# Seven expert groups instead of nine in the last mixture-of-experts layer of a two-block network

## Chip, cores and metric

The kernel runs on one core of one Trainium2 chip. The metric is the device time in microseconds (us) of one execution; the figure for a kernel is the median of its runs.

## What is computed

The program runs a first block of two layers (neighbourhood attention with a Fourier mixer, then a retention mixer, each followed by a mixture of experts) and a second block of one layer (windowed attention, a gated scan and projections) over 256 tokens of 1024 numbers; the first layer also carries 256 context tokens. The part that matters here is the mixture of experts of the second layer, which sees the 256 tokens alone:

```python
def moe_ffn(tok, router_w, router_b, w1, w3, w2):
    T = tok.shape[0]
    scores = jax.nn.sigmoid((tok @ router_w).astype(jnp.float32))
    biased = (scores + router_b.astype(jnp.float32)).reshape(T, N_GROUPS, EXPERTS_PER_GROUP)
    group_score = lax.top_k(biased, TOP_K)[0].sum(axis=-1)
    g_sel = jnp.argmax(group_score, axis=-1)
    ...
    for e in range(N_EXPERTS):
        hid = jax.nn.silu(tok @ w1[e]) * (tok @ w3[e])
        out = out + gate[:, e:e + 1] * (hid @ w2[e])
    return out
```

Each token goes to two of 16 experts (512 places in all). An expert has w1 and w3 of 1024 x 512 and w2 of 512 x 1024 in float32, 6 MB together, and all 16 experts' weights are read once: 96 MB.

## The kernel before

`moe_late` (L1288 on) is the last layer's mixture of experts. It doesn't multiply every token by every expert. Tokens are gathered into rows of a 128-row tile, the products are made for the tile, and the result rows are added back to their tokens. A table, `GROUPS[1]` (L42 to L45), says which experts share a tile and how many of its 128 rows each has. Experts 14 and 15 are fixed: they have places of their own whatever the router says. The other 14 stand by rank: 0 is the expert with most tokens, 13 the one with fewest, found at run time (`ranking`, L1485 on). Before, the table has nine groups: 15 alone with 128 rows, 14 alone with 128 rows, ranks 0 and 13 with 96 and 32, ranks 1 and 12 with 96 and 32, and five pairs with 64 and 64. `CAPS` (L47) keeps the row count of each rank. If an expert has more tokens than rows, `overflow` (L1532 on) runs a loop over all 16 experts under a branch (L1548) that all engines test; it computes the rows that found no place.

Work on a group goes like this. `loads` (L1300) issues its weights on SP's queue: for each of w1, w3 and w2, in two halves, one load of 1 MB for each expert of the group, so a single expert has 6 loads, a pair 12, and a group of three has 18. `expert_load` takes the place of a ranked expert from a register that SP reads from the tile `order` (`places_of`, L1480 to L1483); experts 14 and 15 need no register. The tiles of the loads come from a ring of 11 buffers of 1 MB (3 kept through the program, and 8 of this stage), so load n + 11 can start when the matmuls on load n are done. On TensorE, `products` (L1396 to L1404, the matmul is L1403) goes through a half of a weight in steps of 128 rows of the contraction. At each step it multiplies column blocks of the stationary tokens with the weights of the experts they belong to; the block is as wide as the group's smallest expert (`columns`, L1389): one block of 128 columns for a single expert, two of 64 for a pair of 64s, four of 32 for 96 and 32. So a group is six units: two halves of w1, two of w3 and two of w2, and each unit uses one load for each expert of the group.

Around the products of a group lie, on TensorE, the gather of the next batch's tokens (L1382, four chunks of 8 matmuls for a batch), the slot numbers (L1357), the transposes of the hidden rows (L280) and the scatter of the group before (L1409) into four accumulators. `BATCHES` (L46) says which groups are gathered together, at most two. The weights of the first two groups (`first`, L1306, the first `NS` = 2 groups, 12 loads) are issued ahead of the router. `overflow` is called when group 1 is done, `bias_setup` of the block behind (L1737 on; it writes a table to memory and copies it there, L1759) when group 2 is done. After the last group come the last scatter, the residual and statistics (L1605, L493), and the second block's first product (L220).

Of the kernel before, what the change touches and what calls it, by code (L numbers as in the profile page):

```python
# [18 lines left out]
P = 128  # L19
# [19 lines left out]
NS = 2  # L39
one, two = lambda r: ((r, 128),), lambda a, b: ((a, 64), (b, 64))  # L40
SPLIT = (0, 2, 4, 7, 10, 12)
GROUPS = ((one(15), one(14), one(0), two(8, 13), one(1), one(2), two(9, 12), one(3), one(4), two(10, 11), one(5),  # L42
           one(6), one(7)),
          (one(15), one(14), ((0, 96), (13, 32)), ((1, 96), (12, 32)), two(2, 11), two(3, 10), two(4, 9), two(5, 8),
           two(6, 7)))  # L45
BATCHES = ((0, 1), (2, 3), (4, 5), (6, 7), (8,))  # L46
CAPS = [[dict(x for g in gs for x in g)[r] for r in range(16)] for gs in GROUPS]  # L47


# [81 lines left out]
class Kern:  # L131
# [1156 lines left out]
    def moe_late(self, ss):  # L1288
# [4 lines left out]
        with ExitStack() as es:  # L1293
# [6 lines left out]
            def loads(g):  # L1300

                rs = [r for r, _ in GR[g]]
                return [[load(name, r, u, n, c) for r in rs]
                        for name, n, c in (("moe_w1", 8, 512), ("moe_w3", 8, 512), ("moe_w2", 4, 1024)) for u in range(2)]

            first = [loads(g) for g in range(NS)]  # L1306
            tl, places, gates, rows, nat = self.route(l, ss, rp)
            self.holds = []
            pos, posm = places()
# [15 lines left out]
            def batch(gs):  # L1325
                oh, w = choose(gs)
                return wp.tile([P, KC, 256], F32, tag="xe", name=self.name("xe")), oh, w

            cur = batch(BATCHES[0])
            pm, oi, ranked = self.ranking(tl, pos, NT, lambda: tl([NT, 16, 16]))  # L1330
            ranked(place, posm, V)
            rows()
            g, den = gates()
# [17 lines left out]
            def slots(g, oh, a):  # L1351

                ex = GR[g]
                sp = self.psum((P, 2, 4))
                for i, (r, _) in enumerate(ex):
                    for t in range(NT):
                        nc.tensor.matmul(sp[:, i], oh[:, t, a:a + P], pr4[:, r, t, :], start=t == 0, stop=t == NT - 1)  # L1357
                st = wp.tile([P, 4], F32, tag="slot", name=self.name("slot"))
                a = 0
                for i, (r, n) in enumerate(ex):  # L1360
                    for b in range(a, a + n, 32):

                        c = b + (n if n in (64, 128) else 32)
                        if n in (64, 128) and b > a:
                            continue
                        V.tensor_copy(st[b:c], sp[b:c, i])
                    a += n
                fg = wp.tile([P, 2], F32, tag="fg", name=self.name("fg"))
                V.tensor_scalar(out=fg[:, 0:1], in0=st[:, 1:2], scalar1=-4096.0, scalar2=4096.0, op0=OP.mult, op1=OP.add)
                V.tensor_tensor(out=fg[:, 0:1], in0=fg[:, 0:1], in1=st[:, 0:1], op=OP.add)  # L1370
                V.tensor_tensor(out=fg[:, 1:2], in0=st[:, 2:3], in1=st[:, 3:4], op=OP.add)
                back = wp.tile([P, N], F32R, tag="back", name=self.name("back"))
                V.tensor_scalar(out=back, in0=iota, scalar1=fg[:, 0:1], scalar2=None, op0=OP.is_equal)
                return fg[:, 1:2], back

            def gather(x, oh, w, c):

                ps = self.psum((P, 2, 256))
                for j in range(2):
                    k = 2 * c + j  # L1380
                    for i in range(2 * NT):
                        nc.tensor.matmul(ps[:, j, 0:w], nat[i % 2][:, i // 2, k * P:(k + 1) * P], oh[:, i // 2, 0:w],  # L1382
                                         start=i == 0, stop=i == 2 * NT - 1)
                if c % 2:
                    V.tensor_copy(x[:, 2 * c:2 * c + 2, 0:w], ps[:, :, 0:w])
                else:
                    nc.scalar.activation(x[:, 2 * c:2 * c + 2, 0:w], ps[:, :, 0:w], AF.Copy)
# [8 lines left out]
            def products(outs, lhs, ws, g):  # L1396

                m = ws[0][0].shape[1]
                for u, we in enumerate(ws):
                    for k in range(m):  # L1400
                        for c, ps in enumerate(outs):
                            for a, b, e in columns(g):
                                nc.tensor.matmul(ps[a:b], lhs(u * m + k)[:, a:b], we[e][:, k, 512 * c:512 * c + 512],  # L1403
                                                 start=u == k == 0, stop=u == len(ws) - 1 and k == m - 1)  # L1404

            def scatter(y, back, start, stop):
                for k in range(KC):
                    for i in range(2):
                        nc.tensor.matmul(acc[k // 2][:, k % 2], y[i][:, k * P:(k + 1) * P], back,  # L1409
                                         start=start and k % 2 == i == 0, stop=stop and i == 1, skip_group_check=True)  # L1410
# [3 lines left out]
            todo = None  # L1414
            for bi, gs in enumerate(BATCHES):
                x, oh, _ = cur
                nxt = batch(BATCHES[bi + 1]) if bi + 1 < len(BATCHES) else None
                chunks = list(range(4)) if nxt else []
                for i, g in enumerate(gs):
                    if g >= NS:  # L1420
                        self.places_of(order, oi, GR[g])
                    ws = loads(g) if g >= NS else first[g]
                    xs = lambda k: x[:, k, P * i:P * i + P]
                    h1 = self.psum()
                    products([h1], xs, ws[0:2], g)
                    hs = wp.tile([P, 512], F32, tag="hid", name=self.name("hid"))
                    nc.scalar.activation(hs, h1, AF.Silu)
                    if chunks:
                        gather(*nxt, chunks.pop(0))
                    h3 = self.psum()  # L1430
                    products([h3], xs, ws[2:4], g)
                    V.tensor_tensor(out=hs, in0=hs, in1=h3, op=OP.mult)
                    if todo:
                        scatter(*todo, g == 1, False)
                    gate, back = slots(g, oh, P * i)
                    if len(gs) == 1 and chunks:
                        gather(*nxt, chunks.pop(0))
                    tp = self.psum((P, 4, P))
                    for j in range(4):

                        self.T(tp[:, j, :], hs[:, j::4])
                    hT = wp.tile([P, 4, P], F32, tag="hh", name=self.name("hh"))
                    nc.scalar.activation(hT, tp, AF.Copy)
                    while chunks and (len(gs) == 1 or len(chunks) > 2 * (1 - i)):
                        gather(*nxt, chunks.pop(0))
                    yp = [self.psum() for _ in range(2)]
                    products(yp, lambda k: hT[:, k], ws[4:6], g)
                    y = [wp.tile([P, D], F32R, tag=f"y{j}", name=self.name("y")) for j in range(2)]
                    for c in range(2):
                        s = slice(512 * c, 512 * c + 512)  # L1450
                        nc.scalar.activation(y[0][:, s], yp[c], AF.Copy, scale=gate)
                        V.scalar_tensor_tensor(out=y[1][:, s], in0=yp[c], scalar=gate, in1=y[0][:, s].bitcast(F32),
                                               op0=OP.mult, op1=OP.subtract)
                    todo = y, back
                    if g == 1:
                        c4 = lambda a: a.rearrange("p (k c) -> p k c", c=P)
                        t1 = lambda tag, w: wp.tile([P, w], F32, tag=tag, name=self.name("ov"))
                        room = (c4(t1("y0", D)), t1("y1", D), c4(t1("ovm", 256)), t1("hid", 512), c4(t1("hh", 512)),
                                t1("back", 256), t1("ovs", 64), rp.tile([P, 2, 512], F32, name="ovw"))
                        self.overflow(l, N, NT, cnt, pk, nat, acc, hs[:, 0:1], room, wp)  # L1460
                    if g == 2:
                        with self.pool("bias", 1) as bp:
                            self.bias_setup(bp)
                cur = nxt
# [612 lines left out]
```

## Time and profile before

| | |
|---|---|
| median of 3 runs | 1736.21 us (1733.53 to 1737.06) |
| profiled execution | 1734.04 us, its span 1732.3 us |
| TensorE (PE) busy | 1636.9 us, 94% of the span |
| VectorE, ScalarE, GpSimd busy | 50%, 37%, 15% |
| weight loads of the experts (both layers) | 192 of 1 MB |
| stage of the last layer's experts | from about 1024 us to 1281 us of the span |

The profile is one execution, seen by the hardware's records. Busy time says how long an engine worked, not what the end waited for. So the page's 40 slices show where the stage lies, the table of busy time by stretch shows each group with its DMA share and GB/s, the timeline of TensorE shows what runs in which order and how long, and the queue's own waits show what the loads wait for. A granted clock of 1.00 is TensorE at 2.4 GHz, 0.50 is 1.2 GHz.

### The profile page before, as it was taken

To read this page: it belongs to the slowest core of one execution; us is meant where nothing else is said; L and a number is where in the kernel's file an instruction comes from. 1 tells how busy PE (TensorE), PEld (TensorE's weight loads), DVE (VectorE), ACT (ScalarE), POOL (GpSimd) and SP (SyncE) were. 2 spreads that over 40 slices of the span, in tenths; PEclk is the share of its full clock that TensorE was granted. 3 is DMA by queue.
4 is the path that set the end of the run, shared out by engine and by line. 5 is a ranking of instruction groups with operands and counts; after the bars stand their busy time and mean duration, and the time that the engine had idled before them with its cause. 6 is when DMAs were issued, how large, how long until landed. Compare 5 with 4: busy or idle time off the path is not lost.

```text
span 1732.3 us, 26549 instructions
## 1 busy us (share of the span) xinstructions
PE 1636.9 (94%) x10640; PEld 1222.9 (71%) x10640; DVE 874.4 (50%) x1676; ACT 643.6 (37%) x1008; POOL 266.0 (15%) x265
## 2 busy tenths in 40 slices
PE   5999999988999998999999989999989999999999
PEld 3676657665555455879899955343449999999899
DVE  6565554573424346644555442111135756677665
ACT  3343333333423244433434331010135555655543
POOL 2212101221111111201211020000012110123300
PEclk8999999898999999999999989999989999999999
DMA  9644654477999987354433467999975454433360
GB/s 312 151 134 147 209 187 167 147 311 254 400 384 380 394 326 282 121 194 148 147 122 122 146 252 239 410 420 420 420 257 179 141 159 161 160 122 122 122 214 25
DMA packets 179230, 390.00 MB, mean 225 GB/s; under 512 B 25063, under 2 KB 141864, under 8 KB 149850
## 3 DMA queue, kind: packets, MB, share of 16 engines
q1 hardware_dynamic: 173882, 375.83, 60.1%
q0 software_dynamic: 4336, 10.99, 2.4%
q8 instruction: 87, 1.43, 0.3%
q10 hardware_dynamic: 880, 1.38, 0.2%
q14 instruction: 45, 0.37, 0.1%
HBM read 381.50 MB, written 14.85 MB: 229 GB/s over the span
## 4 chain that ended last, share of the span: by engine, by line
PE 66%; DVE 6%; issue 2%; ACT 2%; POOL 1%; DMA 1%; POOLq 0%; ACTq 0%; DVEq 0%
PE ps L220 12%; PE ps L221 12%; PE ps L222 12%; PE ps L1403 11%; PE ps L1174 8%; PE ps L280 3%; PE ps L1382 1%; DVE wl L211 1%; PE ps L1409 1%; DVE X L1956 1%; PE ps L408 1%; PE ps L1970 1%; DMA w<-in_moe_w_dram 1%; PE ps L1858 0%; PE ps L1839 0%
## 5 line engine op out<-in xcount | busy, mean ns | idle before, releaser
L211 DVE TENSOR_TENSOR wl<-w,wh 128x1024 fp32r<-128x1024 f32 x278 | 346.3, 1261 | 167.3 <-ACT wh L208 165.8
L208 ACT ACTIVATE wh<-w 128x1024 fp32r<-128x1024 f32 x280 | 290.9, 1056 | 200.2 <-PE ps L221 93.1
L220 PE MATMUL ps<-wh,xh 128*128 128x256 f32 x512 | 146.7, 286 | 1.6 <-DVE qk L553 1.6
L221 PE MATMUL ps<-wl,xh 128*128 128x256 f32 x512 | 144.8, 283 | 0.0
L222 PE MATMUL ps<-wh,xl 128*128 128x256 f32 x512 | 144.7, 283 | 0.0
L1403 PE MATMUL ps<-w,xe 128*64 128x512 f32 (+2 forms) x640 | 136.8, 595 | 0.0
L1174 PE MATMUL ps<-w,xe 128*64 128x512 f32 (+1 forms) x320 | 103.6, 596 | 1.2 <-DMA w<-in_moe_w_dram 1.2
L220 PE MATMUL ps<-x,wh 128*128 128x256 f32 x352 | 102.3, 291 | 0.0
L220 PEld LDWEIGHTS ps<-wh,xh 128*128 128x128 f32 x512 | 98.1, 192 | 5.7 <-issue 2.7
L221 PE MATMUL ps<-x,wh 128*128 128x256 f32 x352 | 99.8, 283 | 0.0
L222 PE MATMUL ps<-x,wl 128*128 128x256 f32 x352 | 99.8, 283 | 0.0
L221 PEld LDWEIGHTS ps<-wl,xh 128*128 128x128 f32 x512 | 98.2, 192 | 0.2
L222 PEld LDWEIGHTS ps<-wh,xl 128*128 128x128 f32 x512 | 98.2, 192 | 0.0
L1403 PEld LDWEIGHTS ps<-w,xe 128*64 128x64 f32 (+2 forms) x640 | 43.4, 131 | 72.9 <-issue 70.4
L220 PE MATMUL ps<-xh,wh 128*128 128x512 f32 (+1 forms) x224 | 83.2, 380 | 3.4 <-ACT xh L541 3.0
L221 PE MATMUL ps<-xl,wh 128*128 128x512 f32 (+1 forms) x224 | 82.7, 371 | 1.6 <-DVE xl L542 1.1
L222 PE MATMUL ps<-xh,wl 128*128 128x512 f32 (+1 forms) x224 | 81.4, 364 | 0.9 <-DVE wl L211 0.9
L1174 PEld LDWEIGHTS ps<-w,xe 128*64 128x64 f32 (+1 forms) x320 | 38.3, 158 | 57.5 <-issue 54.6
L220 PEld LDWEIGHTS ps<-x,wh 128*128 128x128 f32 x352 | 67.1, 191 | 1.4
L221 PEld LDWEIGHTS ps<-x,wh 128*128 128x128 f32 x352 | 67.3, 191 | 1.2 <-issue 0.2
L220 PE MATMUL ps<-wh,xp 128*128 128x256 f32 x224 | 65.5, 292 | 2.3 <-ACT xp L1659 2.3
L222 PEld LDWEIGHTS ps<-x,wl 128*128 128x128 f32 x352 | 67.2, 191 | 0.4
(472 smaller groups left out, 3669.8 us busy)
## 6 DMA issues: line engine op xcount, KB each, us to landing
w<-in_moe_w_dram SPq DMA_DIRECT2D x192, 1024.0 KB, 11.6
w<-in_w_in_dram SPq DMA_DIRECT2D x48, 1024.0 KB, 5.0
w<-in_ada_w_dram SPq DMA_DIRECT2D x40, 1024.0 KB, 5.1
w<-in_ret_w_in_dram SPq DMA_DIRECT2D x24, 1024.0 KB, 5.2
w<-in_mixab_w_in_dram SPq DMA_DIRECT2D x10, 1024.0 KB, 6.2
w<-in_ada_w_dram SPq DMA_DIRECT2D x16, 512.0 KB, 8.4
w<-in_ret_w_out_dram SPq DMA_DIRECT2D x8, 1024.0 KB, 5.1
w<-in_mixab_w_out_dram SPq DMA_DIRECT2D x4, 1024.0 KB, 7.4
```

The costliest lines, as they stand in the source:

```text
L208: nc.scalar.activation(hi, t[:, b:b + hk], AF.Copy)
L211: eng.tensor_tensor(out=lo, in0=t[:, b:b + hk], in1=hi.bitcast(F32), op=OP.subtract)
L220: mm(ps, lh, rh, start=start, stop=False, skip_group_check=skip)
L221: mm(ps, lh, rl, start=False, stop=False, skip_group_check=skip)
L222: mm(ps, ll, rh, start=False, stop=stop, skip_group_check=skip)
L280: self.nc.tensor.transpose(out, in_, self.ident[:n, :n])
L408: nc.tensor.matmul(ps[32 * j:32 * j + 32, :], self.S[:, kc, :], w[:, j * 512:(j + 1) * 512], start=kc == 0, stop=kc == KC - 1)
L1174: nc.tensor.matmul(ps[a], x[0][:, q, a], t[:, k, s], start=first, stop=last)
L1382: nc.tensor.matmul(ps[:, j, 0:w], nat[i % 2][:, i // 2, k * P:(k + 1) * P], oh[:, i // 2, 0:w], start=i == 0, stop=i == 2 * NT - 1)
L1403: nc.tensor.matmul(ps[a:b], lhs(u * m + k)[:, a:b], we[e][:, k, 512 * c:512 * c + 512], start=u == k == 0, stop=u == len(ws) - 1 and k == ...
L1409: nc.tensor.matmul(acc[k // 2][:, k % 2], y[i][:, k * P:(k + 1) * P], back, start=start and k % 2 == i == 0, stop=stop and i == 1, skip_gr ...
L1956: mul = lambda e, o, i1: e.tensor_tensor(out=o, in0=o, in1=i1, op=OP.mult)
```

## The change

The table for the last layer has seven groups. The two fixed experts are a pair with 64 rows each. Rank 0 and rank 13 stay with 96 and 32. Rank 1 has 64 rows and shares its tile with ranks 12 and 11, 32 rows each; rank 2 has 64 rows and shares with ranks 10 and 9, 32 rows each. Ranks 3 to 8 make three pairs. The first batch is the first group alone, and the loads issued ahead of the router are those of the first group, again 12. Slot numbers have room for three experts.

```diff
-          (one(15), one(14), ((0, 96), (13, 32)), ((1, 96), (12, 32)), two(2, 11), two(3, 10), two(4, 9), two(5, 8),
-           two(6, 7)))
-BATCHES = ((0, 1), (2, 3), (4, 5), (6, 7), (8,))
+          (two(15, 14), ((0, 96), (13, 32)), ((1, 64), (12, 32), (11, 32)), ((2, 64), (10, 32), (9, 32)), two(3, 8),
+           two(4, 7), two(5, 6)))
+BATCHES = ((0,), (1, 2), (3, 4), (5, 6))
...
-            first = [loads(g) for g in range(NS)]
+            first = loads(0)
...
-                sp = self.psum((P, 2, 4))
+                sp = self.psum((P, 3, 4))
...
-                    if g >= NS:
+                    if g:
                         self.places_of(order, oi, GR[g])
-                    ws = loads(g) if g >= NS else first[g]
+                    ws = loads(g) if g else first
```

On SP's queue, where the loads are issued, the twelfth load (w_8804 is the last of the 12 that are issued ahead of the router) is followed by the branch on the overflow count (cnti). Before:

```order
L192 DMA w_8802<-in_moe_w_dram 128x2048
L192 DMA w_8804<-in_moe_w_dram 128x2048
L1546 TENSOR_LOAD cnti_9211
L1546 ISA x2
L1548 COMPARE_AND_BRANCH
```

The change, at the same place:

```order
L192 DMA w_8802<-in_moe_w_dram 128x2048
L192 DMA w_8804<-in_moe_w_dram 128x2048
L1482 TENSOR_LOAD order_8884
L192 ISA
L192 DMA w_9179<-in_moe_w_dram 128x2048
```

Twelve loads with a rank's register (two reads of `order`) now stand between the twelfth load and the branch. The branch comes behind the 24th load, in the change:

```order
L192 DMA w_9199<-in_moe_w_dram 128x2048
L192 ISA
L192 DMA w_9201<-in_moe_w_dram 128x2048
L1546 TENSOR_LOAD cnti_9379
L1546 ISA x2
L1548 COMPARE_AND_BRANCH
```

On TensorE, at the first group's first product (ps_9037 before, ps_9039 now) and the gather behind it, before:

```order
L1382 MATMUL ps_9017<-oh_8866,nat_8856 128x256
L1403 MATMUL ps_9037<-w_8782,xe_8871 128x512 x4
L1403 MATMUL ps_9037<-w_8784,xe_8871 128x512 x4
L1382 MATMUL ps_9048<-oh_9027,nat_8855 128x256
L1382 MATMUL ps_9048<-oh_9027,nat_8856 128x256
```

The change, from the second half of the same product on:

```order
L1403 MATMUL ps_9039<-w_8786,xe_8871 64x512
L1403 MATMUL ps_9039<-w_8788,xe_8871 64x512
L1403 MATMUL ps_9039<-w_8786,xe_8871 64x512
L1403 MATMUL ps_9039<-w_8788,xe_8871 64x512
L1382 MATMUL ps_9058<-oh_9027,nat_8855 128x256
L1382 MATMUL ps_9058<-oh_9027,nat_8856 128x256
```

Each step of the contraction is now a matmul of 64 columns for each of two experts, so one unit uses two loads where it used one.

## Rows read from the trace of the kernel before

**Rows 1.** The page: its head, and parts of its 40 slices.
```profile
span 1732.3 us, 26549 instructions
...
PE   5999999988999998999999989999989999999999
...
DMA  9644654477999987354433467999975454433360
```

**Rows 2.** Busy time by stretch, one for each group: busy (count), clock, DMA share, GB/s.
```profile
1024.00:1048.30 24.30, 23.57 (x73) 12.01 (x73) 5.03 (x20) 3.78 (x6) 1.43 (x4) 1.00 0.59 203
1048.30:1076.30 28.00, 27.65 (x105) 15.52 (x104) 7.00 (x29) 3.88 (x7) 0.00 (x0) 1.00 0.77 255
1076.30:1107.60 31.30, 30.18 (x231) 10.75 (x230) 5.36 (x15) 3.17 (x5) 0.57 (x1) 1.00 0.87 352
1107.60:1136.50 28.90, 27.77 (x233) 11.28 (x232) 5.37 (x20) 3.17 (x5) 0.56 (x1) 1.00 1.01 410
1136.50:1165.50 29.00, 27.87 (x137) 12.23 (x136) 3.90 (x10) 3.17 (x5) 0.00 (x0) 1.00 1.01 420
1165.50:1194.50 29.00, 27.87 (x137) 12.24 (x136) 4.40 (x14) 3.17 (x5) 0.00 (x0) 1.00 1.01 420
1194.50:1224.60 30.10, 28.97 (x138) 12.36 (x137) 3.63 (x10) 2.95 (x5) 0.00 (x0) 1.00 1.01 420
1224.60:1254.60 30.00, 28.86 (x138) 12.29 (x137) 3.63 (x10) 2.95 (x5) 0.00 (x0) 1.00 1.01 420
1254.60:1280.80 26.20, 24.60 (x113) 9.29 (x112) 1.71 (x7) 1.88 (x3) 1.22 (x4) 1.00 0.85 328
```

**Rows 3.** TensorE's timeline: start, length, line, operation, tiles, count, idle time before.
```profile
1024.18 7.05 PE L1403 MATMUL ps<-w,xe 128*128 128x512 f32 x16
1030.66 1.51 PE L1382 MATMUL ps<-oh,nat 128*128 128x256 f32 x8
...
1073.89 2.47 PE L1409 MATMUL ps<-back,y 128*128 128x256 f32 x16 [0.30 <-PEq L1548]
...
1078.41 7.08 PE L1403 MATMUL ps<-w,xe 128*32 128x512 f32 x64
...
1273.73 7.14 PE L1403 MATMUL ps<-w,hh 128*64 128x512 f32 x32 [0.75 <-ACT hh L1443]
...
1290.72 1.20 PE L1643 MATMUL ps<-c_main,rstd 128*128 128x128 f32 x4 [3.69 <-DVE rstd L1638]
```

**Rows 4.** What SP's queue waited for, 960 to 1290 us: total, times, longest.
```profile
SPq L192 <- PE ps L1403: 197.2, 65, 20.8
```

**Rows 5.** SP's queue: load 12 (L192), the branch (L1548), and when order was ready.
```profile
L192 SPq DMA_DIRECT2D w<-in_moe_w_dram x1: 328/328/328, 1027.8 to 1027.8; - x1
...
L1548 SPq EVENT_SEMAPHORE  x16: 17/17/17, 373.9 to 1033.5; - x16
L1548 SPq COMPARE_BRANCH  x2: 50/52/53, 371.1 to 1028.8; - x2
...
L1502 DVE TENSOR_SCALAR order<-r x2: 157/161/165, 349.0 to 1021.7; 128x16 int32<-128x16 f32 x2
```

**Rows 6.** Loads of L192 issued from 1070 to 1075 us, issue to landing.
```profile
DMA to landing us min/median/max: 5.3/5.8/6.2
```

**Rows 7.** Busy time by stretch again: ahead of and within the saturated part.
```profile
1120.00:1260.00 140.00, 134.33 (x700) 57.63 (x694) 19.36 (x54) 14.21 (x23) 0.00 (x0) 1.00 1.01 420
1027.00:1090.00 63.00, 61.92 (x288) 30.97 (x290) 10.75 (x47) 7.53 (x12) 0.00 (x0) 1.00 0.71 248
```

**Rows 8.** DMA issues, 1000 to 1330 us: the copy of the bias table.
```profile
bD<-bD POOLq DMA_DIRECT2D x1, 1536.0 KB, 9.5
```

**Rows 9.** TensorE's clock behind the stage: a stretch, and two matmuls of L221.
```profile
1288.80:1299.00 10.20, 6.56 (x29) 6.29 (x30) 8.61 (x18) 6.88 (x14) 5.69 (x7) 0.50 0.63 152
...
1294.02 0.41 PE L221 MATMUL ps<-wl,xp 128*128 128x256 f32 x1
...
1301.84 0.28 PE L221 MATMUL ps<-wl,xp 128*128 128x256 f32 x1
```

## Prediction

> **What bounds the kernel now.** The page comes first: TensorE is busy in nearly every slice from the second on, and DMA is at 9 tenths from the 26th to the 29th [rows 1]. Slices are 43.3 us, so those four lie between 1083 and 1256 us, where the last layer's experts run. The second view is busy time by stretch, one stretch for each of the nine groups [rows 2]. By the sums of the nine rows TensorE is busy for 247 of 257 us at a clock of 1.00. The DMA share goes from 0.59 under the first single expert to 1.01 under the pairs, where 420 GB/s stays the same for five groups. So before the change both stand close together: TensorE sets the time of a group (24.3 us for a single, 29.0 for a pair), and a pair's 12 loads at 420 GB/s (1,048,576 bytes each, 2.50 us) take 30.0. The third view is SP's queue: its loads wait for the matmuls that still read a buffer, 65 times [rows 4]. That says who leads: before the change, loads wait for TensorE, not the reverse, and the timeline shows no wait for weights. Bandwidth lies idle at the start only, where single experts ask for less: 248 GB/s from 1027 to 1090 us [rows 7].
>
> **The change, part by part.** Times are of the profiled execution, 1734.04 us, span 1732.3; the median of the runs is 2.2 us above it. In the trace the products end at 1273.73 + 7.14 = 1280.9 us [rows 3]. What lies behind them (last scatter, residual, statistics, first matmul of the next block) starts from their end and isn't changed. So the gain is how much earlier the products end, if the rest follows.
>
> *TensorE's own work.* A unit costs the same whatever the number of experts: two units of a single expert are 16 rows in 7.05 us, two units of 96 and 32 are 64 rows in 7.08 [rows 3], because four blocks of 32 columns run in the time of one of 128. So a group of three costs what ranks 1 and 12 cost, 28.9 us. Group by group now: (15, 14) is the first single plus two more gather chunks of at most 1.51 us [rows 3], as its batch stands alone: 24.3 + 3.0 = 27.3. The second takes the second group's 28.0 (the branch stands behind it, as before), the third 31.3 (with the bias table), the fourth and fifth 28.9 and 29.0, the last two 26.2 each, since no batch is left to gather [rows 2]. The sum is 196.9 us against 256.8 in the nine rows. By TensorE alone the products would end 60 us earlier, at about 1221 us.
>
> *The loads.* Not a byte goes: 96 loads before, 96 after. Eleven have buffers ahead of the first product; the twelfth goes out when the first unit is done, 1027.8 us [rows 5]. Since then 85 loads are to come. Before, they had until 1281; now TensorE frees two buffers a unit from the start instead of one, and the queue is full at once. The narrower first gather (128 columns instead of 256) saves at most some tenths; I take 0.4 and start at 1027.4. A load alone needs 5.3 us to land [rows 6], the 84 behind it 2.50 each at 420 GB/s [rows 7], which is 210.0, and the bias table's copy of 1536 KB shares the engines [rows 8]: at the same rate 3.7 us. The 96th lands at 1027.4 + 5.3 + 210.0 + 3.7 = 1246.4. Its unit takes half of 7.14, 3.6 us. The products end at **1250.0**, 29 us later than TensorE alone would allow: the stage becomes bound by DMA, and the gain is **30.9** of the 60 us.
>
> *The rate against a page.* The five rows of 410 to 420 GB/s [rows 2] say what one core gets here. The Trainium skill, DMA: Bandwidth & Descriptors, Specifications, gives about 358 GB/s as the HBM limit of one core (its section on bandwidth says that this holds when both cores of a memory stream, and gives 425 for one alone). By 358 a load is 2.93 us, an estimate from that page, 84 of them 246, and the products would end at 1286, 5 us later than now. The rows decide for 420.
>
> *Where TensorE waits.* The fourth group, the second of three experts, needs 18 loads, 45 us, for 28.9 us of work; the third's wait is smaller, as loads ran ahead under (15, 14). So TensorE idles some 16 us in all, in pieces of up to 4 us. What a wait does to the clock shows behind the stage: after a wait of 3.69 us [rows 3] the granted clock is 0.50 for 10.2 us and a matmul of 0.28 us takes 0.41 [rows 9]. The Trainium skill, TensorE: Matmul & The Clock Gate, HAM oscillation, tells of a kernel whose waits for DMA at each step keep the clock low, which speaks against this change; by it TensorE would be late in every unit of the group. At half clock a unit is 7.1 us and its share of the other work (28.9 less six units of 3.54, over six, doubled) 2.6: 9.7 against 7.5 us for its three loads, so up to 13 us late at the end of a group that is cold throughout. A TensorE without waits gets its clock back, and the pairs behind give back 1.0, 3.8 and 3.8 us (30.0 less 29.0, 26.2 and 26.2). The bounds are 0 and 13 - 8.6 = 4.4 us, and 11 if the third group's last two units (7 us) are cold too. I take 1, near the lower end, as a cold unit is itself busy nearly all the time.
>
> *SP's queue.* The branch cost SP 4.7 us (1028.8 to 1033.5) [rows 5] with nothing behind it but loads. It now stands behind load 24, which goes out when the second group's first unit is done: 1023.8 + 27.3 + 3.5 = 1054.6. By then loads up to the 20th have landed and more than three, 7.5 us, are under way, which hides 4.7. If it doesn't, 0 to 4.7 us are lost for good; I take 0. The registers of ranks are now wanted from 1027.4 on; `order` is ready at 1021.7 [rows 5]. Slot numbers for three, fewer scatters (7 instead of 9) and VectorE's selections lie beside the loads and cost nothing while DMA leads. The next block's first two weight loads stand behind the 96th and land by 1251.4. The next block's matmuls come 1294.0 - 1280.9 = 13 us behind the products' end [rows 9], so near 1263: a cover of over 10 us, and what it lacked would show as a wait at L220.
>
> *Sum.* 30.9 - 1 = 30 us: 1704 for the profiled execution, **1706** against the median.
>
> **The rivals.**
> - *Cold TensorE or a hole in the loads.* The clock stays at 0.50 through both groups of three, or SP's branch leaves DMA idle: 5 to 15 of the 30.9 us are lost (11 and 4.7 at most), 1710 to 1720. For it speaks [rows 9]; against it that loads run ahead by up to eight buffers, so late TensorE alone doesn't stop DMA.
> - *DMA doesn't lead.* The products follow TensorE: 60 us, 1676. It needs 84 loads in some 181 us, 2.15 us each, 488 GB/s; no stretch shows more than 420.
> - *The page's 358 GB/s.* 5 us slower, 1741. Against it: 420 with a DMA share of 1.01 over 140 us [rows 7].
> - *Overflow, the slow side.* The row limits shrink: experts 14 and 15 from 128 to 64, rank 1 from 96 to 64, ranks 9 to 11 from 64 to 32. One token over a limit turns the branch at L1548, and the loop reads 16 experts twice (once for each 128 tokens), 201 MB, 480 us at 420 GB/s even without waits: about 2190. In the trace of before the branch passes in 0.30 us [rows 3]. By the reference on its seed-0 inputs, experts 14 and 15 get 40 and 24 tokens, and the ranks 73, 64, 45, 44, 39, 33, 23, 23, 20, 20, 17, 17, 17, 13. All fit, rank 1 exactly (64 of 64): one token more there decides.
> - *No less work on the critical path.* If the loads had been the bound throughout, fewer groups would change nothing: 1736. The first two rows (203 and 255 GB/s) speak against it [rows 2].
>
> **How the numbers follow.** Forecast (26 to 35 us gained) 0.76; cold clock or hole 0.13; DMA not leading 0.02; page's rate 0.01; overflow 0.03; nothing changes 0.02; a cost I don't see, of either sign, 0.03. About 0.2%, 3.5 us, is what a measurement of this kernel can tell from no change. Faster 0.93, same 0.02, slower 0.05. The low end is the forecast with every load at the best rate and a start 1.5 us earlier, 35 us: 1701, and 1 for the runs' spread, 1700. The high end takes in most of the cold case: 1717.
>
> **What would show it.** In the profile after: DMA share about 1.01 and 420 GB/s from about 1030 to 1246 us without a gap; products ending near 1250; TensorE idle for weights (L1403 waiting on the load) mostly in the second group of three, with some stretches at clock 0.50; a group of three's units at 3.5 us each when warm; the distance from the products' end to the next block's first matmul still some 13 us. Wrong would be: a gap in DMA behind the 24th load; products ending after 1258; a unit of three dearer than 3.5 us at full clock; instructions of the overflow loop; or a new wait at L220.

## The result and the profile after

| | before | changed kernel |
|---|---|---|
| median of 4 runs each, on one chip | 1734.87 us (1732.46 to 1737.06) | 1715.80 us (1712.12 to 1718.76) |
| ratio, 95% interval | | 0.9889 [0.9864, 0.9915] |
| profiled execution, its span | 1734.04, 1732.3 us | 1718.76, 1717.0 us |
| first product to last product of the stage | 256.7 us | 238.5 us |

The change is faster by 19.1 us. The forecast was 30. The page of the changed kernel, against [rows 1]: the DMA row has its 9s from the 26th to the 29th slice as before, with an 8 on either side where a 7 stood, and TensorE's row falls to 7 in the 26th and the 30th. "DMA; 6%" stands in the chain of waits, under the experts' loads.

```profile
span 1717.0 us, 26370 instructions
...
PE   5999999988999999999999989789979999999999
...
PEclk8999999898999999899999979899989999999999
DMA  9644654377999996353533468999985444533360
...
PE 24%; DMA 6%; DVE 3%; issue 2%; ACT 1%; POOL 1%; POOLq 0%; ACTq 0%; SPq 0%; DVEq 0%
```

Busy time by stretch, one row for each of the seven groups (columns as in [rows 2]):

```profile
1026.98:1055.60 28.62, 28.62 (x137) 12.00 (x136) 5.75 (x28) 3.17 (x6) 0.29 (x2) 0.91 0.76 307
1055.60:1092.40 36.80, 26.27 (x234) 10.86 (x232) 6.49 (x24) 3.86 (x6) 0.00 (x0) 0.92 0.92 372
1092.40:1127.90 35.50, 34.34 (x250) 14.81 (x252) 6.29 (x22) 3.17 (x5) 1.12 (x2) 0.94 0.91 371
1127.90:1177.30 49.40, 39.77 (x235) 12.85 (x234) 4.06 (x11) 3.17 (x5) 0.00 (x0) 0.97 1.01 417
1177.30:1207.70 30.40, 28.92 (x141) 12.44 (x140) 3.90 (x10) 3.17 (x5) 0.00 (x0) 1.00 1.01 420
1207.70:1238.00 30.30, 27.15 (x124) 11.22 (x123) 3.21 (x9) 2.57 (x4) 0.00 (x0) 1.00 1.01 420
1238.00:1265.50 27.50, 24.65 (x107) 9.16 (x106) 1.78 (x8) 1.88 (x3) 1.22 (x4) 1.00 1.02 403
```

From the fourth group on this is the profile that was forecast. DMA is full at 420 GB/s. Pairs with 12 loads take 30.4 and 30.3 us (2.5 us a load). The group with 18 takes 49.4: 45.0 for its loads at that rate, and the bias table's copy falls into this stretch (issued at 1125.4, landed 10.7 us later). TensorE is idle for some 10 of the 49.4 us. The queue's waits over 960 to 1290 us say who leads now. Where loads waited for matmuls 65 times [rows 4], it is 35 times, and 52 waits are for a load itself. SP marks the landings of its loads with eight semaphores in turn, and from load 51 on nearly every load waits, on its own semaphore, until the load issued eight places before it has landed; the matmuls that held its buffer are done by then. The last line is the branch's own waits, to which we come below.

```profile
SPq L192 <- DMA w<-in_moe_w_dram: 99.1, 52, 4.3
SPq L192 <- PE ps L1403: 88.8, 35, 24.5
...
SPq L1548 <- SPq L1548: 8.5, 5, 2.7
```

TensorE waits for loads as well, 12 times (its waits over 1015 to 1285 us):

```profile
PE ps L1403 <- DMA w<-in_moe_w_dram: 11.3, 12, 1.8
```

The first three groups aren't as forecast: 307, 372 and 371 GB/s where 420 was possible. Two holes and a late start make that up. **The late start** is in TensorE's timeline:

```profile
1026.98 9.59 PE L1403 MATMUL ps<-w,xe 128*64 128x512 f32 x32
...
1037.63 7.09 PE L1403 MATMUL ps<-w,xe 128*64 128x512 f32 x32
...
1074.78 7.08 PE L1403 MATMUL ps<-w,hh 128*32 128x512 f32 x64
1092.41 3.78 PE L1409 MATMUL ps<-back,y 128*128 128x256 f32 x16 [10.54 <-issue]
...
1098.61 7.07 PE L1403 MATMUL ps<-w,xe 128*32 128x512 f32 x64
...
1257.78 7.70 PE L1403 MATMUL ps<-w,hh 128*64 128x512 f32 x32 [0.75 <-ACT hh L1443]
```

The first 32 matmuls take 9.59 us, the next 32 of the same shape 7.09. The clock tells why. It stood at 0.50 for 23.8 us at the head of the stage in the changed kernel, and for 17.0 before (second row, of the kernel before):

```profile
1008.20:1032.00 23.80, 18.39 (x69) 11.79 (x70) 18.39 (x72) 10.13 (x21) 6.76 (x11) 0.50 0.75 307
```

```profile
1005.50:1022.50 17.00, 10.76 (x43) 7.71 (x44) 14.49 (x54) 8.67 (x19) 5.18 (x7) 0.50 1.02 416
```

So the first buffers come free late. Load 12, which waits for them, goes out 54.6 us after the stage's first load (1033.16 less 978.55). Before it was 51.0 (1027.83 less 976.85). Of these 3.6 us, 1.1 lie ahead of the first product (1026.98 and 1024.18) and 2.5 behind it, in the first unit.

**The first hole** is SP's. The rows are SP's queue and the other engines at line 1548 from 1055 to 1095 us, and the loads from 1058 to 1070:

```profile
L1548 SPq EVENT_SEMAPHORE  x8: 17/17/17, 1060.8 to 1069.1; - x8
L1548 SPq COMPARE_BRANCH  x1: 53/53/53, 1060.3 to 1060.3; - x1
L1548 PEldq COMPARE_BRANCH  x1: 6932/6932/6932, 1079.6 to 1079.6; - x1
...
L192 SPq DMA_DIRECT2D w<-in_moe_w_dram x2: 332/342/353, 1059.3 to 1069.7; - x2
...
DMA to landing us min/median/max: 9.8/9.8/9.8
```

Load 24 goes out at 1059.3 and lands 9.8 us later, at 1069.1. SP's test takes 53 ns at 1060.3; then come eight waits on semaphores, the last at 1069.1, and load 25 follows at 1069.7. The semaphores are those of the loads: the waits for loads 21 to 24 end at 1061.5, 1063.9, 1066.6 and 1069.1, one landing after the other. SP leaves the branch only when every load that it has issued has landed. The queue of loads is empty by then.

**The second hole** is TensorE's. Its test of the same branch starts at 1079.6, 2.3 us before the products of the group are done (1074.78 + 7.08 = 1081.86), and lasts 6.93 us. The scatter follows at 1092.41, after 10.54 us of idle time. Before it was 0.30 [rows 3]. The clock falls in that time too, to 0.50 from 1086.7 to 1096.9, so that the scatter's 16 matmuls take 3.78 us (2.18 in the group before). No buffer comes free, so SP has nothing to issue from 1082.5 to 1101.4, and the loads run dry. Busy time in both holes and at the cold scatter (last three columns: clock, DMA share, GB/s):

```profile
1066.00:1070.00 4.00, 4.00 (x44) 1.24 (x40) 0.00 (x0) 0.00 (x0) 0.00 (x0) 1.00 0.37 147
1070.00:1074.00 4.00, 4.00 (x35) 3.23 (x28) 1.65 (x9) 0.06 (x1) 0.00 (x0) 1.00 0.79 258
...
1090.00:1094.00 4.00, 1.59 (x7) 1.59 (x8) 0.00 (x0) 0.00 (x0) 0.00 (x0) 0.50 1.00 414
...
1098.00:1102.00 4.00, 4.00 (x38) 1.54 (x40) 0.00 (x0) 0.60 (x1) 0.00 (x0) 1.00 0.27 113
1102.00:1106.00 4.00, 4.00 (x40) 1.30 (x32) 0.00 (x0) 0.26 (x1) 0.00 (x0) 1.00 0.87 295
```

Against 420 GB/s the first hole lacks (273 + 162) x 4 us = 1.74 MB and the second (307 + 125) x 4 = 1.73 MB, that is 4.1 us each.

### The profile page after: what moved, and what is told of

Read it like the earlier page. It is cut to its first block, busy times and chain, and to the rows that moved or that the text cites. A ratio compares the mean times of both kernels' runs of the same rounds, so it can differ in the third digit from the quotient of the medians.

```text
span 1717.0 us, 26370 instructions
## 1 busy us (share of the span) xinstructions
PE 1600.5 (93%) x10568; PEld 1199.6 (70%) x10568; DVE 866.4 (50%) x1658; ACT 637.4 (37%) x998; POOL 266.5 (16%) x265
## 5 line engine op out<-in xcount | busy, mean ns | idle before, releaser
L220 PE MATMUL ps<-wh,xh 128*128 128x256 f32 x512 | 146.6, 286 | 1.6 <-DVE qk L553 1.6
L221 PE MATMUL ps<-wl,xh 128*128 128x256 f32 x512 | 144.7, 283 | 0.0
L1403 PE MATMUL ps<-w,xe 128*32 128x512 f32 (+1 forms) x640 | 115.1, 616 | 10.2 <-DMA w<-in_moe_w_dram 10.2
L220 PE MATMUL ps<-x,wh 128*128 128x256 f32 x352 | 102.2, 290 | 0.0
L220 PEld LDWEIGHTS ps<-wh,xh 128*128 128x128 f32 x512 | 98.1, 192 | 5.7 <-issue 2.7
L221 PE MATMUL ps<-x,wh 128*128 128x256 f32 x352 | 99.7, 283 | 0.0
L221 PEld LDWEIGHTS ps<-wl,xh 128*128 128x128 f32 x512 | 98.2, 192 | 0.2
L220 PE MATMUL ps<-xh,wh 128*128 128x512 f32 (+1 forms) x224 | 83.3, 381 | 3.9 <-ACT xh L541 3.7
L1403 PEld LDWEIGHTS ps<-w,xe 128*32 128x32 f32 (+1 forms) x640 | 31.6, 124 | 79.1 <-issue 56.9
L221 PE MATMUL ps<-xl,wh 128*128 128x512 f32 (+1 forms) x224 | 82.9, 372 | 1.2 <-DVE xl L542 1.1
L1174 PEld LDWEIGHTS ps<-w,xe 128*64 128x64 f32 (+1 forms) x320 | 37.8, 158 | 58.9 <-issue 54.6
L220 PEld LDWEIGHTS ps<-x,wh 128*128 128x128 f32 x352 | 67.1, 191 | 1.4
L221 PEld LDWEIGHTS ps<-x,wh 128*128 128x128 f32 x352 | 67.2, 191 | 1.2 <-issue 0.2
L220 PE MATMUL ps<-wh,xp 128*128 128x256 f32 x224 | 65.6, 293 | 2.1 <-ACT xp L1659 2.1
```

The lines of the kernel that those rows point to most:

```text
L220: mm(ps, lh, rh, start=start, stop=False, skip_group_check=skip)
L221: mm(ps, lh, rl, start=False, stop=False, skip_group_check=skip)
L1174: nc.tensor.matmul(ps[a], x[0][:, q, a], t[:, k, s], start=first, stop=last)
```

## The experiments

Theory: the loads lead from the second group on, at 2.50 us each, and the forecast's missing part lies in the branch (two holes) and in the cold start. Rivals: TensorE's pace or its clock leads; the groups of three cost more than was thought; the branch costs nothing and something else is slower.

The table gives each kernel's median, its ratio to the kernel before on the same chip, and three pieces of the stage in the kernel's profile: from its first load to load 12 (SP's queue), from there to the end of the last product, and on to the next block's first matmul (L220). The rest of the program, median less the sum, is 1413 to 1419 us in every row. These 6 us do not follow the edits, so small differences are read from the stage.

| kernel | median us | ratio, 95% interval | to load 12 | to last product | to L220 | sum |
|---|---|---|---|---|---|---|
| before | 1734.87 | | 51.0 | 253.0 | 12.8 | 316.8 |
| changed kernel | 1715.80 | 0.9889 [0.9864, 0.9915] | 54.6 | 232.3 | 13.3 | 300.2 |
| e0_again | 1715.20 | 0.9882 [0.9865, 0.9899] | 54.6 | 232.3 | 13.3 | 300.2 |
| e1_branch_last | 1712.16 | 0.9866 [0.9849, 0.9883] | 54.6 | 224.2 | 17.4 | 296.2 |
| e2_no_branch | 1706.14 | 0.9838 [0.9822, 0.9855] | 54.6 | 225.3 | 13.1 | 293.0 |
| e3_nine_branch_last | 1728.05 | 0.9952 [0.9933, 0.9970] | 51.1 | 245.9 | 14.5 | 311.4 |
| e4_pair_only | 1721.36 | 0.9933 [0.9913, 0.9954] | 54.4 | 239.4 | 13.7 | 307.6 |
| e5_threes_only | 1729.07 | 0.9972 [0.9957, 0.9988] | 51.1 | 249.1 | 13.5 | 313.7 |
| e6_two_thirds | 1679.93 | 0.9690 [0.9671, 0.9709] | 54.6 | 199.3 | 13.0 | 266.9 |
| e7_branch_first | 1714.76 | 0.9888 [0.9872, 0.9904] | 54.0 | 232.6 | 12.8 | 299.4 |
| e8_warm | 1713.97 | 0.9890 [0.9874, 0.9907] | 49.4 | 225.0 | 22.2 | 296.6 |
| e9_warm_mid | 1709.56 | 0.9860 [0.9844, 0.9877] | 49.5 | 226.7 | 14.2 | 290.4 |
| e10_nine_no_branch | 1728.11 | 0.9964 [0.9951, 0.9977] | 51.3 | 246.2 | 13.6 | 311.2 |
| e11_warm_no_branch | 1704.75 | 0.9831 [0.9815, 0.9847] | 49.5 | 224.6 | 12.8 | 286.8 |

### e0_again: the changed kernel once more

> The changed kernel once more, for a second profile and a base on the same chip. Theory B (branch): SP's test of the overflow branch behind the 24th load takes 8.9 us (1060.3 to 1069.2 in the first profile) because SP waits there until its loads under way have landed, and TensorE's own branch behind the second group takes 10.5 us idle time; each leaves DMA without work for some 4 us (GB/s falls to 147 and 113 in 4 us stretches). Both holes must stand at the same places again; 1713 to 1718 us. Rival C (clock): the missing 11 us come from TensorE at clock 0.50 at the stage's start (until 1032.05 in the first profile) and in its waits; then the time must follow that stretch from profile to profile and the holes vary. Rival D (rate): loads land more than 2.50 us apart while DMA share is 1.01.

1715.20 us, and the same three pieces to 0.1 us. Line 1548 holds TensorE again, for 9.94 us of idle time. So the stage's length is a property of the kernel, not of one execution.

### e1_branch_last and e2_no_branch: the branch moved, and left out

```diff
...
-                    if g == 1:
+                    if g == NG - 1:
...
```

> The same overflow, called when the last group is done instead of the second. Theory B: both holes go, as no expert load is queued behind SP's test any more and TensorE's branch has nothing but the last scatter behind it; two holes of 4 us and what a late TensorE adds, 7 to 10 us less than the changed kernel, 1705 to 1709 us, with DMA share about 1.01 from 1035 us to the last load. Rivals C and D: no change by more than 2 us, 1714 to 1718.

In e2_no_branch the call of `overflow` is taken out.

> The overflow and its branch left out (rows beyond an expert's limit would not be computed). Theory B: the same as with the branch behind the last group, within 2 us, 1704 to 1709. If it is faster than that by more than 3 us, the branch costs behind the last group too. Rivals C and D: 1714 to 1718.

e1_branch_last has 1712.16 us, 3.0 under e0_again (the intervals of the two overlap) and not the 1705 to 1709 expected. e2_no_branch has 1706.14, inside its range, and is 6.0 under e1: by what was said before the run, the branch costs behind the last group too. With the branch in the last group the products end 8.1 us sooner after load 12 (224.2 against 232.3). Without it they end 7.0 us sooner, and there is no hole: 419 GB/s from 1031 to 1230 us.

```profile
1031.00:1230.00 199.00, 181.24 (x1106) 72.80 (x1104) 27.53 (x85) 19.01 (x30) 1.13 (x2) 0.99 1.01 419
```

So the two holes, 8.2 us by the arithmetic above, are the branch's, and 7 to 8 us of the stage. What each hole costs by itself no run shows. At the end of the stage the branch isn't free, which is one reason why e1 missed its range. TensorE's timeline of e1_branch_last shows the gap, and the way to the next block grows from 13.3 to 17.4 us:

```profile
1241.58 7.94 PE L1403 MATMUL ps<-w,hh 128*64 128x512 f32 x32 [0.75 <-ACT hh L1443]
1252.96 3.57 PE L1409 MATMUL ps<-back,y 128*128 128x256 f32 x16 [3.44 <-PEq L1548]
```

### e3_nine_branch_last and e10_nine_no_branch: the same in the nine groups

> The kernel before, nine groups, with the overflow called when the last group is done. Theory B: the branch costs where loads lead only; with nine groups TensorE leads and its branch took 0.30 us, so no change against the kernel before: -2 to +1 us. If the branch costs by itself wherever it stands, it would be 7 to 10 us faster here too, 1725 to 1728.

> The kernel before with the overflow left out (rows beyond an expert's limit are not computed). Theory (the branch costs the nine groups some 5 us at load 12 and, at the last group, 3 us of TensorE): 1722 to 1727 us, that is, 1 to 5 under e3_nine_branch_last, and the seven groups without it (1706) are 16 to 21 us faster, so the branch takes a little more from the changed kernel (9) than from the one before (8 to 12). Rival (the branch cost nothing in the kernel before, and e3_nine_branch_last was faster by something else): 1733 us or more.

The edit is that of e1 and of e2, in the kernel before. The branch cost the nine groups too: 1728.05 with it in the last group and 1728.11 without it, against 1735.95 and 1733.86 for the kernel before on the same chips, and 5.4 to 5.6 us of the stage. My expectation for e3, no change, was wrong, and e10 came out 1 us over its range. Of the time, the branch costs 6 to 8 us in the nine groups (0.0036 of it by e10's ratio, 0.0048 by e3's) and 9 in the seven (1715.20 less 1706.14). Without it the change is worth 22 us (1728.11 less 1706.14; the quotient of the two ratios gives the same). By group, the second, third and fourth take 25.2, 27.5 and 26.2 us in e10 where they took 28.0, 31.3 and 28.9, and the fifth 31.2 where it took 29.0; TensorE has the same matmuls in both. Why those groups are shorter isn't shown.

### e4_pair_only and e5_threes_only: each half of the change

```diff
...
+          (two(15, 14), ((0, 96), (13, 32)), ((1, 96), (12, 32)), two(2, 11), two(3, 10), two(4, 9), two(5, 8),
+           two(6, 7)))
...
```

> The two fixed experts as a pair, no groups of three: eight pairs. Theory (each load costs 2.50 us once the queue is full; the overflow's branch holds TensorE some 10 us and empties SP's queue; the first unit runs cold): TensorE needs 8 groups of about 28.3 us = 226, plus 10 at the branch, plus 3 cold = 239 us from the first product to the last, against 238.5 in the changed kernel and 256.7 before, so nearly all of the gain is here: 1714 to 1720 us. Rival (the groups of three bring the gain, a third of the products less for six experts): half of it or less, 1725 us or more.

```diff
...
+          (one(15), one(14), ((0, 96), (13, 32)), ((1, 64), (12, 32), (11, 32)), ((2, 64), (10, 32), (9, 32)),
+           two(3, 8), two(4, 7), two(5, 6)))
...
```

> Groups of three, but the two fixed experts each by itself as before: eight groups. Theory: the first 24 loads are metered by TensorE's two single groups, 2 x 24.3 = 48.6 us from the first product, then 72 loads at 2.50 us = 180, plus 5.3 for the first landing and 3.7 for the last products = about 238 to 243 us from the first product to the last (256.7 before): 1717 to 1724 us. The branch comes behind load 12 as before, where one load is under way. The clock at the start should be at half for 17 us as before and not 24. Rival (TensorE's sum decides: 2 x 24.3 and 6 x 28.3 = 218 us): 1700 us or less. Rival (threes bring nothing, their products being bound by loads anyway): 1733 us or more.

The pair alone gives 9.2 us of the stage, the threes alone 3.1, both 16.6. Neither median fell where I had put it: 1721.4 for 1714 to 1720, 1729.1 for 1717 to 1724. The waits say why the halves are worth less by themselves. With the pair alone TensorE still leads: the queue waits for matmuls, twice for a load, and its eight groups fill the stage, seven of 27 to 32 us each and the second, with the branch behind it, of 39.9.

```profile
SPq L192 <- PE ps L1403: 188.6, 57, 24.4
...
SPq L192 <- DMA w<-in_moe_w_dram: 4.3, 2, 3.8
```

With the threes alone it is the loads that lead later on (TensorE waited 12 times for a load, 11.1 us), but the two single experts have held them back for two groups first. The pair lets the loads start, the threes let TensorE keep up with them.

### e6_two_thirds: fewer loads, the same products

```diff
...
-                        for name, n, c in (("moe_w1", 8, 512), ("moe_w3", 8, 512), ("moe_w2", 4, 1024)) for u in range(2)]
+                        for name, n, c in (("moe_w1", 8, 512), ("moe_w3", 8, 512)) for u in range(2)]
...
```

> Left out: every load of w2; the product with w2 reads w3's tiles instead, so that 64 loads of 1 MB are left of 96 while TensorE's products stay as they are; the branch stands in the last group. Theory (the loads decide from the second group on): TensorE is freed to its own pace, 7 groups of about 28.3 us = 198 plus 3 cold = 201 to 206 us from the first product to the last, against 230.3 with all loads: some 25 us less than with the branch in the last group alone, 1683 to 1692 us. Rival (TensorE's pace or its clock decides, and the waits for loads only take the place of it): no change, 1708 to 1714 us.

1679.93 us, ratio 0.9690 [0.9671, 0.9709]: 32 us under e1_branch_last, and 3 below the range. From the first product to the last are 205.4 us (230.3 in e1_branch_last), within the 201 to 206 of the theory. That the loads lead in the seven groups is shown. The whole was shorter than expected as the branch cost TensorE only 0.18 us here: the way to the next block is 13.0 us, where e1 has 17.4.

### e7_branch_first: the branch behind the first group

```diff
...
-                    if g == 1:
+                    if g == 0:
+                        scatter(*todo, True, False)
+                        todo = None
...
```

> The changed kernel with the overflow behind the first group, its count turned into an integer ahead of the groups: SP meets the branch ahead of load 12, when all of its loads have landed, and TensorE meets it between the first and the second group. Theory: SP has nothing to wait for, so no hole in the loads; TensorE's stop of 4 to 10 us comes while 5 loads or more are under way and while the loads still lead, and is caught up with at some 2 us a group: as without the branch, 1705 to 1709 us, 7 to 11 under the changed kernel. Rival (the stop of TensorE holds back releases, and the loads lose as much): 1711 to 1716 us. Rival (SP waits for the count until the first group is done): 1725 us or more.

1714.76 us, no gain: the first rival. Load 12 had gone out before the branch after all, since it stands with the first twelve, so SP waited for its landing (1031.1 to 1035.4):

```profile
L1553 SPq EVENT_SEMAPHORE  x8: 17/17/17, 1031.6 to 1035.4; - x8
L1553 SPq COMPARE_BRANCH  x1: 53/53/53, 1031.1 to 1031.1; - x1
```

TensorE's test took 6.05 us at a DMA share of 1.02, with almost nothing of its own to do beside it, and the loads ran dry behind it as in the changed kernel (162 GB/s from 1064 to 1068 us, 291 to 1072).

```profile
1054.66:1060.71 6.05, 0.62 (x6) 0.42 (x4) 0.00 (x0) 0.00 (x0) 0.00 (x0) 0.83 1.02 418
```

### e8_warm, e9_warm_mid and e11_warm_no_branch: a warm start

All three have idle products between TensorE's small pieces of work ahead of the stage (`warm`, called at five places, 19 products in all and not the 20 of the expectations; `self.wz` is a tile that nobody reads):

```diff
...
+    def warm(self, rhs, n=1):
+        for _ in range(n):
+            self.nc.tensor.matmul(self.wz[:, 0:256], self.ident, rhs, start=True, stop=True, skip_group_check=True)
...
```

> e1_branch_last with 20 idle products of 128x256 on TensorE, whose result nobody reads, set between its small pieces of work from the end of the block before to the first gather, so that it doesn't lie still there. Theory (the clock falls to half because TensorE has only small pieces in these 15 us, and the cold gather and first unit start the queue of loads late): the clock stays at full speed or falls for less than 10 us, the gather of 32 products takes about 3.7 instead of 6.5 us, the first unit 7.1 instead of 9.5, load 12 is issued some 4 to 6 us sooner after the block before, and as the loads decide from there on, the whole is that much shorter: 1705 to 1709 us against 1712 of e1_branch_last. Rival (the cold first unit is covered by the loads, or the idle products delay the chain of small steps by as much): 1711 us or more.

In e9_warm_mid the call of `overflow` stands ahead of `gate, back = slots(...)` of the last group.

> As e8_warm, and the overflow in the last group between its second and its third product instead of behind the third. Theory: behind the last product TensorE's branch stood bare (3.44 us); between the second and the third TensorE waits for DVE, ACT and the last loads anyway (0.85, 0.75 and 1.24 us in e1_branch_last), so 1 to 3 us of the branch are hidden: 1 to 3 us under e8_warm. Rival (the branch takes longer there, as it did in the changed kernel while loads were under way: 6.9 us and not 3.4): 2 us over e8_warm or more.

> The changed kernel without the overflow (rows beyond an expert's limit are not computed), as e2_no_branch, and with the 20 idle products of e8_warm. It shows what the cold clock at the head of the stage costs, without the branch, whose length varied from kernel to kernel. Theory (the stream of loads starts with the first released buffers, and each us sooner there is a us at the end): from load 1 to the next block 287 to 289 us against 293.0 in e2_no_branch, as load 12 came 5.2 us sooner after load 1 in e8_warm than in e1_branch_last: 1700 to 1703 us. Rival (the head of the stage is hidden behind the loads, and the idle products bring nothing): 292 us or more there, 1705 to 1708 us.

The clock stayed at 1.00 and the gather of 31 matmuls took 3.68 us (stretch and timeline of e8_warm):

```profile
1003.00:1028.00 25.00, 22.00 (x129) 14.91 (x129) 20.81 (x79) 11.12 (x23) 8.52 (x14) 1.00 0.87 341
```

```profile
1019.75 3.68 PE L1400 MATMUL ps<-oh,nat 128*128 128x128 f32 x31 [1.08 <-DVE nat L571]
...
1025.53 5.37 PE L1421 MATMUL ps<-w,xe 128*64 128x512 f32 x24 [0.23 <-DVE xe L1403]
...
1257.81 3.58 PE L1427 MATMUL ps<-back,y 128*128 128x256 f32 x16 [5.38 <-issue]
```

Load 12 comes 5.2 us sooner after the first load, and the products' end follows it. e8_warm gave this back at its branch, where TensorE stood for 5.38 us and ran cold behind it (22.2 us to the next block): 1713.97, not the 1705 to 1709 expected. e9_warm_mid doesn't meet that: its test lasted 3.35 us beside products that were still queued, the stage is 9.8 us shorter than the changed kernel's, and with 1709.56 us, 4.4 under e8_warm where 1 to 3 were expected, it is the fastest kernel here that keeps the overflow. Its interval overlaps that of e0_again between 0.9865 and 0.9877, so that it beats the changed kernel is likely, and that it beats the one before is plain. Without the branch the warm start takes 6 us from the stage (286.8 against 293.0), as the theory has it, but the medians, of two chips, differ by 1.4 us only, 1704.75 against 1706.14, and 1704.75 lies above the 1700 to 1703 expected. The stage shows the cold start's cost; that the whole time keeps it isn't shown.

## Why the prediction was right, and short by a third

The predicted pieces of the stage, from load 1 on, were 50.6 (1027.4 less 976.85), 222.6 (1250.0 less 1027.4) and 12.8 us, 286.0 together. Measured are 54.6, 232.3 and 13.3. The gain in the stage is 16.6 us and not 30.9. The median's 19.1 lies 2.5 above that, within what the rest of the program varies by. So it is in part luck that 1715.8 lies inside the range of 1700 to 1717: the stage's gain alone gives 1718.3 (1734.87 less 16.6). The case held likeliest, 26 to 35 us gained, at 0.76, did not come; what came was the rival at 0.13. And two of the signs that were named as wrong were seen: a gap in DMA behind load 24, and products that end after 1258, at 1265.5.

- **The loads become the bound: right.** Loads land 2.50 us apart at 420 GB/s, and e6 shows that they lead. By the 358 GB/s of the Trainium skill (DMA: Bandwidth & Descriptors, Specifications) there would have been no gain; the rows of the fourth to the sixth group show 417 to 420.
- **A group of three costs what 96 and 32 cost: right.** 64 rows in 7.08 us [rows 3], and 7.08 and 7.07 for the same shape in the changed kernel, for a group of two (1074.78 above) and for a group of three (1098.61).
- **"The branch cost SP 4.7 us … I take 0": the step that failed.** I read 1028.8 to 1033.5 [rows 5] as a fixed price that loads under way would hide. It was a wait for load 12, issued at 1027.8, to land: SP stood at that load's semaphore until 1033.2. A wait for the queue to run empty can't be hidden by what is in the queue: the more is under way, the longer it lasts (8.8 us behind load 24), and a landing's latency is lost afterwards.
- **"The branch stands behind it, as before" for TensorE, 0.30 us: failed too.** The test took 3.65 us before as well, but it began 6.6 us before the products ended, in the shadow of sixteen long matmuls. Behind 64 short ones it began 2.3 us ahead, lasted 6.9, and another 5.9 us went by before the scatter. Both together are the second piece: 7.0 of the 9.7 us that it lacks, by e2 and e0. The other 2.7 stand in e2 too, which has no branch, and have no experiment of their own.
- **"The narrower first gather … I take 0.4": wrong sign.** The stage's head was 4.0 us longer than predicted. The clock was looked for in TensorE's waits in the groups of three, for 1 us; those waits made it fall once, for 3.4 us (0.97 in the row of 49.4 us), and the 0.94 of the other group of three comes from the branch, behind which it began cold. In the kernel that the Trainium skill tells of (TensorE: Matmul & The Clock Gate, HAM oscillation) each wait for DMA made the next step start cold. That didn't happen here, but the 12 waits, of 1.8 us at most, are also shorter than that kernel's. The clock's cost lay at the head, where the first unit ran at half of it, and behind the branch, where it was at half for 10.2 us. The single expert first has 51.1 us (e5), the pair first 54.4 (e4), the pair with a warm start 49.5.
- **The end: right.** 13.3 us behind the products, 12.8 before, and no wait for weights at L220.

With both missed terms taken away, in e11_warm_no_branch, the stage is 286.8 us, where the sum has 286.0. That they are so close is partly chance: the head is 1.1 us shorter than in the sum (49.5 for 50.6) and the products 2.0 longer (224.6 for 222.6). The sum had the right mechanism and left out two prices. The rival "cold TensorE or a hole in the loads", 1710 to 1720 us, is what happened, both at once, though it saw the cold stretch in another place.

## What to carry to other kernels

A branch that every engine tests was cheap here where no load was queued and TensorE still had products to do (0.18 us in e6): look up what its waits end on, above all whether they end when a transfer lands, before moving it into a stretch where transfers are kept queued. When a change lets the transfers lead, each us by which their stream starts late or stands still is lost at the end, so price the start of the stream and each interruption, not only its rate. Two halves of a change can each be worth little where one frees a resource and the other one uses it.

## What the hardware showed that I hadn't expected

- **TensorE's test of a branch lasts longer while DMA is full.** Its time, and the DMA share meanwhile: 3.65 us at 0.14 (before), 3.31 at 0.15 (e5), 3.65 at 0.02 (e6), 3.35 at 0.06 (e9); 4.85 at 0.46 (e3), 5.49 at 0.53 (e8), 6.45 at 0.61 (e1); 6.93, 6.19, 6.07 and 6.05 at 1.01 to 1.02 (changed kernel, e0, e4, e7). The rows of the kernel before and of e6:

```profile
L1548 PEldq COMPARE_BRANCH  x1: 3647/3647/3647, 1067.0 to 1067.0; - x1
...
1066.95:1070.60 3.65, 3.65 (x10) 1.70 (x9) 1.16 (x7) 0.00 (x0) 0.00 (x0) 1.00 0.14 54
```

```profile
L1548 PEldq COMPARE_BRANCH  x1: 3652/3652/3652, 1222.4 to 1222.4; - x1
...
1222.35:1226.00 3.65, 3.65 (x20) 1.14 (x16) 0.00 (x0) 0.39 (x1) 0.00 (x0) 1.00 0.02 4
```

  SP, DVE and ACT test the same branch in 45 to 56 ns. The Trainium skill, Advanced Engine Details and Errata, Control Flow Timing, gives about 108 ns for a compare-and-branch; these three take about half of it, TensorE over 30 times as long. The packets of the DMA queue that the profile's page calls instruction (q8) say what its test ends with. In all 25 tests of the 14 runs, 14 of them in the layer before, a packet of 16 KB moves during the test, and the test ends 1.4 to 1.5 us after the packet. With a DMA share of up to 0.15 the packet starts 0.9 to 1.3 us after the test, with DMA full 3.5 to 4.4 us (in the changed kernel at 1083.99, for 1.07 us; the test ends at 1086.49). The 5.9 us behind the test in the changed kernel (6.1 in e0, 6.2 in e4, 3.0 in e8) end in the same way: a second packet arrives (1089.97, for 1.06 us), and the scatter begins 1.3 to 1.5 us after it, in all four. So it fits that TensorE stands until its instructions have come, through DMA engines that are full of loads. No run held back or hastened such a packet, so the cause is argued and not shown.
- **How far TensorE's sequencer runs ahead depends on the matmuls' shape.** It reached the branch 6.6 us before the products' end with 16 of 128 columns (before, e5), 3.1 to 4.1 with 32 of 64 (e8, e1, e6, e3), 2.3 with 64 of 32 (changed kernel, e0, e4). What fits under a lead of 6.6 us stands bare under one of 2.3.
